# The down products of a feed-forward stage by one level of Strassen's scheme, with the weights streamed in order of use and all tiles at one remainder of 512 bytes

## The chip, the cores and the metric

One NeuronCore of a Trainium2 chip runs the kernel. The metric is the device time of one execution in microseconds; lower is better. TensorE multiplies, VectorE (DVE), ScalarE (ACT) and GpSimd (POOL) do the elementwise work, and SyncE (SP) issues the DMAs.

## The reference

Two decoder layers over 512 tokens of width 1024, in float32. Each layer is a mixer between two half-step SwiGLU feed-forward blocks, every block behind an RMS norm. The mixer is stick-breaking attention (16 heads of 64) in the first layer, and sliding-window attention with sinks and rotary angles in the second.

```
def swiglu(h, w_gate_up, w_down):
    gate, up = jnp.split(h @ w_gate_up, 2, axis=-1)
    return (jax.nn.silu(gate) * up) @ w_down
...
for i in range(DEPTH):
    x = x + 0.5 * swiglu(rms_norm(x, norm_gains[i, 0]), ffn_w_gate_up[i, 0], ffn_w_down[i, 0])
    h = rms_norm(x, norm_gains[i, 1])
    x = x + (stick_breaking_attention if i % 2 == 0 else sliding_window_attention)(h, ...)
    x = x + 0.5 * swiglu(rms_norm(x, norm_gains[i, 2]), ffn_w_gate_up[i, 1], ffn_w_down[i, 1])
```

The inner width of the feed-forward blocks is 2816, which is 22 tiles of 128; the model width is 8 tiles.

## The kernel before

Activations stand transposed: a tile holds 128 features on the partitions and the 512 tokens as columns. The eight tiles `x0` to `x7` hold the residual stream. Every float32 product is made of three passes in the type float32r: an operand is split exactly into a high part (a copy that rounds, on ACT) and a low part (what is left, by a subtraction on DVE), and `terms` issues high x high, high x low and low x high (line 75). The instructions on TensorE stay in the order of the program; the other engines' are ordered by a scheduler when the kernel is built.

The program runs six stages: feed-forward 0, stick-breaking attention, feed-forward 1, feed-forward 2, sliding-window attention, feed-forward 3. All weights form one stream in units of 8 tiles (7 for two in three of the down units). `_load` starts the DMA of a unit into one of three raw buffers (line 158), `_part` splits it (ACT on line 181, DVE on line 186, for some attention units POOL on line 184) into one of three pairs `whi` and `wlo`, and `release` goes on with the next unit when TensorE has used one.

A feed-forward stage (`ffn`) first goes over the 22 columns of 128 inner features. For each it makes two banks `gu` in PSUM, gate and up, each of 8 terms of 512 columns, and `swiglu` (lines 307 to 314) turns them into the parts `hh` and `hl`. Then come the down products: for each of the 8 output tiles one bank `dn` gathers 22 terms, in units of 8, 7 and 7; `residual` adds half of it to `x` (line 300), and `following` hands the tile to `norm_tile` of the next stage (lines 252, 253, 260 and 261: two parts of the tile times its gain, and its squares added to `acc`, by POOL for tiles 1 to 5 and by DVE for 6 and 7). After the last stage `following` stores the tile.

The tiles of the constants, of the weights and normalised activations, and of a stage lie one behind another in SBUF. Three small tiles `nv`, `nr`, `nt` of 16 bytes a partition, 32 in the placement, lie between the second group and the third. So weights and normalised activations begin at 96 bytes over a multiple of 512, and the tiles of the feed-forward and stick-breaking stages at 192.

Of the kernel before, what the change touches and what calls it, by code (L numbers as in the profile page):

```python
# [15 lines left out]
P = 128  # L16
T = 512
# [5 lines left out]
DOWN = (8, 7, 7)  # L23
# [13 lines left out]
NEG = -1.0e30  # L37
ROT = HD // 4
NROT = ROT // 2
# 500000 ** (-arange(0, 16, 2) / 16) in float32  # L40
# [24 lines left out]
class _Ordered:  # L65
    """an engine whose instructions stay in the order of the program"""
# [40 lines left out]

class _Trunk:
    def __init__(self, tc, pools, psum, aps):
        self.tc, self.nc = tc, _Engines(tc)  # L110
        self.const, self.work = pools
        self.psum = psum
        self.aps = aps
        self.units = []
        self.raw, self.ready = [], []
        self.taken = self.spent = 0
        self.roped = False
        self.extra = -1

# [7 lines left out]
    def terms(self, out, pairs, first=True, last=True, release=()):  # L127
# [4 lines left out]
        for i, ((wh, wl), (xh, xl)) in enumerate(pairs):  # L132
# [3 lines left out]
            if i in ((n - 1,) if release == 1 else release):  # L136
                self.release(1)
            yield cost

    def mm3(self, out, pairs, first=True, last=True, release=()):  # L140
        for _ in self.terms(out, pairs, first, last, release):
            pass
# [5 lines left out]
    def queue(self, ap, pool=False):  # L148
        self.units.append((ap, ap.shape[1], pool))

    def _load(self, pieces=1):
        n = len(self.raw)
        if n < len(self.units):
            ap = self.units[n][0]
            raw = self.work.tile([P, ap.shape[1]], F32, tag="raw", name=f"raw{n}", bufs=UNITS)
            self.raw.append(raw)
            if pieces == 1:
                self.nc.sync.dma_start(raw, ap)

    def _open(self, n):  # L160
        size = self.units[n][1]
        hi = self.work.tile([P, size], F32R, tag="whi", name=f"whi{n}", bufs=UNITS)
        lo = self.work.tile([P, size], F32R, tag="wlo", name=f"wlo{n}", bufs=UNITS)
        self.ready.append((hi, lo))

    def advance(self, hi, lo):
        """one more unit of the weight stream ahead, in tiles that the stage has free"""
        n = self.extra = len(self.ready)
        self.ready.append((hi, lo))
        self._part(n)  # L170
        self._load()

    def _part(self, n, i=0, pieces=1):
        nc, (ap, size, pool) = self.nc, self.units[n]
        size //= pieces
        s = slice(i * size, (i + 1) * size)
        hi, lo = self.ready[n]
        raw = self.raw[n]
        if pieces > 1:
            nc.sync.dma_start(raw[:, s], ap[:, s])  # L180
        nc.scalar.copy(hi[:, s], raw[:, s])  # L181
        if pool and pieces == 1:
            for t in (slice(0, size // 2), slice(size // 2, size)):
                nc.gpsimd.tensor_sub(lo[:, t], raw[:, t], hi[:, t])  # L184
        else:
            nc.vector.tensor_sub(lo[:, s], raw[:, s], hi[:, s])  # L186

    def release(self, count):
        self.spent += count
        ahead = UNITS + (self.spent <= self.extra)  # L190
        while count and len(self.ready) < min(self.spent + ahead, len(self.units)):
            n = len(self.ready)
            self._open(n)
            self._part(n)
            self._load()

    def weights(self, a):
        """the next unit of the stream as [row, a, column] high and low parts"""
        hi, lo = self.ready[self.taken]
        self.taken += 1  # L200
        h3, l3 = (t.rearrange("p (a b) -> p a b", a=a) for t in (hi, lo))
        return [(h3[:, i, :], l3[:, i, :]) for i in range(a)]

# [1 line left out]
    def setup(self, which):  # L205
# [10 lines left out]
        for n in range(UNITS):  # L216
            self._load(2)
            self._open(n)
        for half in range(2):
            for m in range(4):  # L220
                k = 4 * half + m
                nc.sync.dma_start(self.x[k], aps["xt"][k])
                if m < UNITS:
                    self._part(m, half, 2)
                self.norm_tile(k, which)
        for _ in range(UNITS):
            self._load()
        self.ident = c.tile([P, P], F32, name="ident")
# [15 lines left out]
    def norm_tile(self, k, which):  # L244
        nc, w = self.nc, self.work
        if k == 0:
            self.xh, self.xl = [], []
# [6 lines left out]
        self.xh.append(hi)  # L254
        self.xl.append(lo)
        if k == 0:
            nc.scalar.activation(self.acc, self.x[k], AF.Square)
        else:
            sq = w.tile([P, T], F32, tag="rbc", name="sq", bufs=1)
            nc.scalar.activation(sq, self.x[k], AF.Square)  # L260
            (nc.gpsimd if k < POOL_SQUARES else nc.vector).tensor_add(self.acc, self.acc, sq)  # L261
# [11 lines left out]
    def norm_rows(self):  # L273
# [4 lines left out]
        v = w.tile([P, TB], F32, tag="nv", name="nv", bufs=1)  # L278
        r = w.tile([P, TB], F32, tag="nr", name="nr", bufs=1)
        tmp = w.tile([P, TB], F32, tag="nt", name="nt", bufs=1)  # L280
# [17 lines left out]

    def residual(self, n, ps, factor):
        self.nc.vector.scalar_tensor_tensor(self.x[n], ps, factor, self.x[n], ALU.mult, ALU.add)  # L300

# [1 line left out]
    def swiglu(self, fp, f, gu):  # L303
        nc = self.nc
        g = fp.tile([P, T], F32, tag="g", name="g", bufs=2)
        u = fp.tile([P, T], F32, tag="u", name="u", bufs=2)
        nc.vector.tensor_mul(g, gu[0], self.rbc)  # L307
        nc.scalar.activation(g, g, AF.Silu)
        nc.vector.tensor_mul(u, gu[1], self.rbc)  # L309
        nc.vector.tensor_mul(u, g, u)  # L310
        hi = fp.tile([P, T], F32R, name=f"hh{f}")
        lo = fp.tile([P, T], F32R, name=f"hl{f}")
        nc.scalar.copy(hi, u)
        nc.vector.tensor_sub(lo, u, hi)
        return hi, lo

    def ffn(self, following, first=False, rope=False):
        tc, nc = self.tc, self.nc
        with tc.tile_pool(name="ffn", bufs=1) as fp:
            hs, evac = [], []  # L320
            xs = list(zip(self.xh, self.xl))
            ahead = []
            if first:
                ahead = [(self.bank("gu"), self.weights(KD)) for _ in range(3)]
                for half in range(2):
# [704 lines left out]
```

## Time and profile before

| | us |
|---|---|
| median of 3 runs | 1927.21 |
| lowest and highest run | 1924.83, 1928.83 |
| span of the profiled execution | 1925.5 |
| feed-forward 1: gate/up, down | 240.89, 123.21 |
| stick-breaking stage | 265.32 |
| sliding-window stage | 190.53 |

The span runs from the first to the last instruction. The page gives no device time for the profiled execution itself; its span lies inside the range of the three runs. The table's stages are stretches between the first matmuls of one kind and of the next. In the profile's rows, PE is TensorE's matmuls, PEld its weight loads; `gu<-xh,whi` reads: the bank `gu` was written from `xh` and `whi`. A matmul's length in a row is that of its pipeline; the distance of two starts is what it costs.

### The profile page before, as it was taken

The numbers are of one execution on the slowest core, as the hardware profiler recorded it, in microseconds if no ns is written. First come the engines' busy times: TensorE is split into PE (matmuls) and PEld (weight loads), VectorE is DVE, ScalarE is ACT, GpSimd is POOL, SyncE is SP. The second block draws the span as 40 slices with busy tenths as digits, with TensorE's granted clock in tenths as the row PEclk, the third lists the DMA queues.
The fourth block names the chain that finished last, engine by engine and source line by source line (L and its number), as shares of the span: only waits on it lengthen the run. The fifth ranks groups of instructions, "written<-read, shape, count | busy, mean of one in ns | idle before, by whom it ended". The sixth has DMA issues, their size and how long they took to land.

```text
span 1925.5 us, 22581 instructions
## 1 busy us (share of the span) xinstructions
PE 1895.7 (98%) x8994; PEld 1565.6 (81%) x8994; DVE 970.5 (50%) x1535; ACT 695.1 (36%) x1071; POOL 172.0 (9%) x131
## 2 busy tenths in 40 slices
PE   9999999999999999999999999999998999999999
PEld 7888888877887888888888888888887788888887
DVE  6444433378887644443235444423588664444321
ACT  5333222266675323332223333222357542223211
POOL 1000000233321000000000000000142210000000
PEclk9999999999999999999999999999989999999999
DMA  5233333321112333223333222333221122332331
GB/s 167 98 97 99 96 91 92 103 69 56 49 62 66 99 97 97 92 97 94 97 96 99 92 98 96 93 93 100 81 67 34 29 92 98 99 99 90 103 109 60
DMA packets 49930, 170.52 MB, mean 89 GB/s; under 512 B 5921, under 2 KB 6177, under 8 KB 49825
## 3 DMA queue, kind: packets, MB, share of 16 engines
q1 hardware_dynamic: 49824, 169.07, 27.9%
q8 instruction: 71, 1.16, 0.2%
q14 instruction: 35, 0.28, 0.0%
HBM read 166.96 MB, written 2.10 MB: 88 GB/s over the span
## 4 chain that ended last, share of the span: by engine, by line
PE 84%; DVE 8%; issue 4%; ACT 3%; POOL 1%; DMA 0%; SPq 0%; ACTq 0%; DVEq 0%; POOLq 0%
PE gu L75 49%; PE dn L75 23%; PE op L75 4%; PE tok L75 3%; DVE keep L459 2%; DVE beta L460 1%; PE pv L75 1%; DVE qs L376 1%; DVE wt L482 1%; ACT keep L453 1%; PE sc L75 1%; PE z L75 0%; PE ptr L75 0%; DVE e L793 0%; PE q L75 0%
## 5 line engine op out<-in xcount | busy, mean ns | idle before, releaser
L181 ACT CAST whi<-raw 128x1024 fp32r<-128x1024 f32 (+2 forms) x323 | 330.0, 1022 | 964.8 <-issue 361.6
L75 PE MATMUL gu<-xh,whi 128*128 128x512 f32 x1400 | 545.5, 390 | 1.4 <-ACT whi L181 1.4
L75 PE MATMUL gu<-xh,wlo 128*128 128x512 f32 x1400 | 545.0, 389 | 0.7 <-DVE wlo L186 0.7
L75 PE MATMUL gu<-xl,whi 128*128 128x512 f32 x1400 | 544.8, 389 | 0.5 <-DVE xl L253 0.5
L186 DVE TENSOR_TENSOR wlo<-raw,whi 128x1024 fp32r<-128x1024 f32 (+2 forms) x293 | 349.4, 1193 | 248.2 <-ACT whi L181 245.6
L75 PEld LDWEIGHTS gu<-xh,wlo 128*128 128x128 f32 x1400 | 262.8, 188 | 56.5 <-DVE wlo L186 1.8
L75 PEld LDWEIGHTS gu<-xh,whi 128*128 128x128 f32 x1400 | 262.9, 188 | 56.2 <-ACT whi L181 1.9
L75 PEld LDWEIGHTS gu<-xl,whi 128*128 128x128 f32 x1400 | 262.9, 188 | 55.3 <-DVE xl L253 0.9
L75 PE MATMUL dn<-hh,wlo 128*128 128x512 f32 x704 | 280.9, 399 | 0.0
L75 PE MATMUL dn<-hl,whi 128*128 128x512 f32 x704 | 277.4, 394 | 0.0
L75 PE MATMUL dn<-hh,whi 128*128 128x512 f32 x704 | 276.0, 392 | 0.0
L309 DVE TENSOR_TENSOR u<-gu,rbc 128x512 f32<-128x512 f32 x87 | 60.1, 691 | 274.7 <-PE gu L75 274.7
L75 PEld LDWEIGHTS dn<-hl,whi 128*128 128x128 f32 x704 | 132.1, 188 | 34.3
L75 PEld LDWEIGHTS dn<-hh,whi 128*128 128x128 f32 x704 | 132.2, 188 | 31.5
L75 PEld LDWEIGHTS dn<-hh,wlo 128*128 128x128 f32 x704 | 132.2, 188 | 30.5
L307 DVE TENSOR_TENSOR g<-gu,rbc 128x512 f32<-128x512 f32 x88 | 60.8, 691 | 176.5 <-PE gu L75 176.4
L261 POOL TENSOR_TENSOR acc<-acc,sq 128x512 f32<-128x512 f32 x30 | 46.4, 1547 | 1116.1 <-ACT sq L260 1116.1
L184 POOL TENSOR_TENSOR wlo<-raw,whi 128x512 fp32r<-128x512 f32 x60 | 87.5, 1483 | 164.9 <-ACT whi L181 164.9
L75 PE MATMUL tok<-whi,xh 128*128 128x256 f32 x288 | 86.4, 300 | 0.0
L75 PE MATMUL tok<-whi,xl 128*128 128x256 f32 x288 | 82.4, 286 | 0.1
L75 PE MATMUL tok<-wlo,xh 128*128 128x256 f32 x288 | 82.3, 286 | 0.1
L300 DVE SCALAR_TENSOR_TENSOR x<-dn,x 128x512 f32<-128x512 f32 x32 | 22.1, 691 | 116.5 <-PE dn L75 116.5
(310 smaller groups left out, 1957.4 us busy)
## 6 DMA issues: line engine op xcount, KB each, us to landing
raw<-in_gu_dram SPq DMA_DIRECT2D x173, 512.0 KB, 3.4
raw<-in_dn_dram SPq DMA_DIRECT2D x64, 448.0 KB, 3.3
raw<-in_dn_dram SPq DMA_DIRECT2D x32, 512.0 KB, 3.5
raw<-in_sbqk_dram SPq DMA_DIRECT2D x16, 512.0 KB, 3.4
raw<-in_swin_dram SPq DMA_DIRECT2D x10, 512.0 KB, 3.5
raw<-in_sbv_dram SPq DMA_DIRECT2D x8, 512.0 KB, 3.3
raw<-in_sbo_dram SPq DMA_DIRECT2D x8, 512.0 KB, 3.5
raw<-in_swo_dram SPq DMA_DIRECT2D x8, 512.0 KB, 3.3
```

The costliest lines, as they stand in the source:

```text
L75: return self._tc.keep_in_program_order(method(*args, **kwargs))
L181: nc.scalar.copy(hi[:, s], raw[:, s])
L184: nc.gpsimd.tensor_sub(lo[:, t], raw[:, t], hi[:, t])
L186: nc.vector.tensor_sub(lo[:, s], raw[:, s], hi[:, s])
L261: (nc.gpsimd if k < POOL_SQUARES else nc.vector).tensor_add(self.acc, self.acc, sq)
L300: self.nc.vector.scalar_tensor_tensor(self.x[n], ps, factor, self.x[n], ALU.mult, ALU.add)
L307: nc.vector.tensor_mul(g, gu[0], self.rbc)
L309: nc.vector.tensor_mul(u, gu[1], self.rbc)
L376: nc.vector.tensor_sub(out[other, h, :], src[own, :], out[own, h, :])
L453: nc.scalar.activation(keep[:, :, :n], z[:, :, :n], AF.Sigmoid, scale=-0.125)
L459: nc.vector.tensor_tensor_scan(rev, rev, rev, 1.0, ALU.mult, ALU.bypass)
L460: nc.vector.tensor_mul(beta[:, :, : n - 1], beta[:, :, : n - 1], keep[:, :, 1:n])
```

## The change

**Down products.** The inner tiles are taken in pairs, even and odd (11 pairs), the output tiles in pairs n and n + 4 (4 blocks), and the 512 tokens in two halves of 256. Each block is then a product of two-by-two matrices, for which Strassen's scheme (in Winograd's form) needs 7 products, where the plain form has 8. It needs sums: of the weights, four per block, made by POOL in `make_sums`; of the activations, three per pair, made by DVE in `swiglu`, which now writes seven operands per pair, high and low, each of 256 columns. The pairs are cut in two halves of the stage, `PAIRED = (6, 5)`: gate/up of 12 columns, down with 6 pairs, gate/up of 10 columns, down with 5 pairs. Each product's bank is added to a half of a tile of `x` as soon as it ends; products 1, 6, 7 and 4 of a block gather in one bank, and 5 and 3 in another, so that a product waits for the evacuation before it in its bank. `norm_tile` follows products 3 and 4 of a block in the second half.

**Stream.** DMA units are of 12 tiles (10 in the second half of a stage) in the order of use; splits are of 6 tiles (5) into one of `SLOTS = 4` slots. There are two raw buffers, and a third in feed-forward stages. `take` hands out single tiles, and `used` frees a slot. The first stage's first units are interleaved by tile, as the first matmuls want them.

**Placement.** The three small tiles move to the constants, and tiles of a few bytes are widened to 512 or put into one such line (`LINE`), so that every tile that TensorE reads from the weights, the normalised activations and a stage begins at one remainder of 512.

The core of the diff:

```diff
-DOWN = (8, 7, 7)
+TILES = 6
+SLOT = TILES * P
+RAWS, MORE_RAWS = 2, 1
+SLOTS = 4
+PAIRED = (6, 5)
+BLOCKS = KD // 2
...
+    def make_sums(self, g, t):
...
+        nc.gpsimd.tensor_add(s[0], a21, a22)
+        nc.gpsimd.tensor_sub(s[1], s[0], a11)
+        nc.gpsimd.tensor_sub(s[3], a12, s[1])
+        nc.gpsimd.tensor_sub(s[2], a11, a21)
...
+    def _split(self, n, s=slice(None), load=None):
...
+        self.nc.scalar.copy(hi, src)
+        if pool:
+            for h in (slice(0, t // 2 * P), slice(t // 2 * P, t * P)):
+                self.nc.gpsimd.tensor_sub(lo[:, h], src[:, h], hi[:, h])
+        else:
+            self.nc.vector.tensor_sub(lo, src, hi)
...
-        hi = fp.tile([P, T], F32R, name=f"hh{f}")
-        lo = fp.tile([P, T], F32R, name=f"hl{f}")
-        nc.scalar.copy(hi, u)
-        nc.vector.tensor_sub(lo, u, hi)
-        return hi, lo
+        if not odd:
...
+            part(0, 1, h[:, 0:1, :])
+            nc.vector.tensor_sub(t[:, 0, :], h[:, 1, :], h[:, 0, :])
+            part(1, 2, t[:, 0:1, :])
+        else:
...
+            part(2, 4, h)
+            nc.vector.tensor_sub(t[:, 1, :], h[:, 1, :], t[:, 0, :])
+            nc.vector.tensor_sub(t[:, 2, :], h[:, 1, :], he[:, 1, :])
+            nc.vector.tensor_sub(t[:, 3, :], h[:, 0, :], t[:, 1, :])
+            part(4, 7, t[:, 1:, :])
...
-            for n in range(KD):
-                ps = self.bank("dn")
-                at = 0
-                for size in DOWN:
-                    self.mm3(ps, list(zip(self.weights(size), hs[at : at + size])), first=(at == 0), last=(at + size == NF), release=1)
-                    at += size
-                self.residual(n, ps, 0.5)
-                following(n)
+    def down(self, pairs, following):
...
+        for n, p in down_order(BLOCKS):
+            out = bank(n, p)
+            j = (1, 5, 2, 3, 6, 7, 4).index(p)
+            first = p in (1, 2, 5)
+            w = self.take(pairs)
+            for i in range(pairs):
+                wh, wl, (slot, _) = w[i]
+                xh, xl = self.ops[i][j]
+                for m, (l, r) in enumerate(((wh, xh), (wh, xl), (wl, xh))):
+                    self.nc.tensor.matmul(out, l, r, ...)
+            for row, col, ps in {
+                1: ((0, 0, out),), 2: ((0, 0, out),), 6: ((0, 1, out),), 3: ((0, 1, out),),
+                7: ((1, 1, out),), 5: ((1, 1, out),), 4: ((1, 0, out),),
+            }[p]:
+                x = self.x[n + BLOCKS * row][:, col * W2 : (col + 1) * W2]
+                self.nc.vector.scalar_tensor_tensor(x, ps, 0.5, x, ALU.mult, ALU.add)
+            if following and p in (3, 4):
+                following(n + BLOCKS * (p == 4))
+            self.used(slot, pairs)
...
+def down_order(blocks):
+    out = []
+    for n in range(blocks):
+        out += [(n, 1), (n, 5)] + ([(n - 1, 4)] if n else []) + [(n, 2), (n, 6), (n, 3), (n, 7)]
+    return out[:-2] + [(blocks - 1, 7), (blocks - 1, 3), (blocks - 1, 4)]
```

Sums for block n + 1 are issued when the last split of block n is; a slot is freed at the end of the product that used it.

More of the change, by code (lines that the diff above doesn't have):

```diff
@@ L166, in advance @@
[L166 to L202, printed above, removed]
+    def queue(self, ap, sizes, pool=False, own=None, special=False):
+        n = len(self.loads)
+        self.loads.append((ap, own))
+        self.reads.append(len(sizes))
+        at = 0
+        for size in sizes:
+            s = slice(at * P, (at + size) * P)
+            self.plan.append((size, lambda s=s: self.raws[n][:, s], (n,), pool, None, special))
+            at += size
@@ L401, in project_pair @@
             ps = self.bank(nm)
-            yield from self.terms(ps, list(zip(self.weights(KD), xs)), release=1)
+            yield from self.terms(ps, list(zip(self.take(KD), xs)))
             if start:
@@ L1006, in layout @@
+    tiles = [t for cc in (CHUNKS, *range(CHUNKS)) for t in sw[cc]]
+    a["ww"] = stream(tiles + out_tiles(sw_w_out), "w")
     a["pos"] = c(np.asarray(positions).reshape(TB, P).T)
```

441 lines of the change are left out of this document (302 added, 139 removed).

## The prediction

> **What bounds the kernel now.** I read the page first (busy shares, then the chain that ended last), then the sums over stretches, cut where the matmuls change from one stage to the next.
>
> ```profile
> span 1925.5 us, 22581 instructions
> PE 1895.7 (98%) x8994; PEld 1565.6 (81%) x8994; DVE 970.5 (50%) x1535; ACT 695.1 (36%) x1071; POOL 172.0 (9%) x131
> PE 84%; DVE 8%; issue 4%; ACT 3%; POOL 1%; DMA 0%; SPq 0%; ACTq 0%; DVEq 0%; POOLq 0%
> ```
>
> TensorE is busy for 98% of the span and carries 84% of the chain; DVE is half idle and POOL nearly idle. The span lies 1.7 us under the median of the runs (1927.21), so I take differences from the trace and add them to the median. About 0.2% (3.9 us) is what a measurement of this kernel can tell from no change.
>
> ```profile
> core 0: us, PE busy (x) PEld busy (x) DVE busy (x) ACT busy (x) POOL busy (x), PEclk, DMA share, GB/s
> 250.32:373.54 123.22, 123.22 (x530) 99.12 (x529) 37.02 (x40) 32.92 (x40) 13.05 (x9) 1.00 0.31 92
> 1798.28:1921.49 123.21, 123.21 (x529) 98.93 (x527) 31.79 (x32) 22.12 (x23) 0.00 (x0) 1.00 0.30 89
> sum 492.85, PE 492.85 PEld 396.27 DVE 147.75 ACT 120.87 POOL 28.96; mean PE 123.21 PEld 99.07 DVE 36.94 ACT 30.22 POOL 7.24
> ...
> 1557.51:1798.28 240.77, 240.77 (x1068) 199.47 (x1066) 114.31 (x149) 74.74 (x94) 0.00 (x0) 1.00 0.30 96
> ```
>
> The first two rows are the first and the last of four down stretches, the sum is over the four; the last row is a gate/up stretch. PE is busy without a break in all of them at the full clock. A down stretch has 528 matmuls of 512 columns, 123.21/528 = 0.2333 us each. A gate/up stretch has 1056 and a few small ones, 0.227 us each. What TensorE has to do in these stages is their time; a gain there is a gain at the end.
>
> **The change part by part.** *Fewer products.* Per pair of output rows, 7 products of half width take the place of 8: 4 blocks x 7 products x 11 pairs x 3 passes = 924 matmuls of 256 columns per stage, 3696 in all, for 2112 of 512. The projections to token rows already run 256 columns with a new weight each time:
>
> ```profile
> 389.75 0.28 PE L75 MATMUL tok<-whi,xh 128*128 128x256 f32 x1
> 389.87 0.28 PE L75 MATMUL tok<-wlo,xh 128*128 128x256 f32 x1
> 389.99 0.28 PE L75 MATMUL tok<-whi,xl 128*128 128x256 f32 x1
> 390.11 0.28 PE L75 MATMUL tok<-whi,xh 128*128 128x256 f32 x1
> ```
>
> The starts stand 0.120 us apart (the 0.28 is the pipelined length). That is not half of 0.227: 2 x 0.120 - 0.227 leaves 0.013 us per matmul that does not shrink with the columns. So 3696 x 0.120 = 443.5 us against 492.85: -49.3, or 12.3 a stage. The ends are half of a down matmul, 0.1167 (-61.5), and half of the old down plus that 0.013, 0.130 (-12.4); I take 0.120, the row of the very shape. The Trainium skill, "TensorE: Matmul & The Clock Gate", section "Back-to-back issue gap", gives columns / 2.4 + 2.5 ns, 109 ns at 256: by that, as an estimate, the new down would be 403 us. The rows of this trace stand above it at both widths, and they decide.
>
> *Placement.* All tiles now begin at one remainder of 512 bytes. Before, weights and normalised activations share one (96) and run at 0.227, while the down products' activations lie at another (192) and run at 0.233. At one common remainder I leave gate/up at 0.227 and have counted 0.120 for down, whose row is of the equal kind. The 192 output-projection matmuls of the stick-breaking stage, also mixed, may gain as much as 0.0063 each: 0 to -1.2; I take -1.
>
> *New work on DVE, ACT and POOL.* Two output rows used to need 44 tiles of weights split into parts, in six splits, and two evacuations of 512 columns. Now they need, in each half, 7 splits (6 tiles wide in the first, 5 in the second: 77 tiles) and 7 evacuations of 256 columns, and POOL makes 4 sums for them.
>
> ```profile
> L186 DVE TENSOR_TENSOR wlo<-raw,whi 128x896 fp32r<-128x896 f32 x64 | 69.9, 1092 | 101.9 <-ACT whi L181 99.6
> L181 ACT CAST whi<-raw 128x896 fp32r<-128x896 f32 x64 | 60.3, 943 | 245.7 <-PE dn L75 217.6 <-PE gu L75 28.1
> L314 DVE TENSOR_TENSOR hl<-u,hh 128x512 fp32r<-128x512 f32 x88 | 60.4, 686 | 4.1 <-ACT hh L313 4.1
> L313 ACT CAST hh<-u 128x512 fp32r<-128x512 f32 x88 | 54.7, 621 | 62.1 <-DVE u L310 62.1
> L840 DVE TENSOR_TENSOR ol<-pv,oh 128x256 fp32r<-128x256 f32 x16 | 6.6, 415 | 7.4 <-ACT oh L839 7.4
> L686 POOL TENSOR_TENSOR q<-ra,rb 128x256 f32<-128x256 f32 x3 | 2.2, 738 | 0.2
> ...
> L184 POOL TENSOR_TENSOR wlo<-raw,whi x60: 1264/1298/2280, 364.9 to 1431.7; 128x512 fp32r<-128x512 f32 x60
> L253 DVE SCALAR_TENSOR_TENSOR xl<-x,gain,xh 128x512 fp32r<-128x512 f32 x7 | 5.2, 744 | 0.0
> ```
>
> Between 512 and 896 columns DVE takes 1.06 ns per column: 0.957 us for 768 (first half, six pairs), 0.821 for 640 (second, five). ACT's copies by its two rows: 0.84 and 0.73, under the 2.16 or 1.80 us of a product, so ACT is no bound. POOL by 256 (0.738) and 512 (median 1.298): 2.19 ns per column, 1.86 and 1.58 a sum. An evacuation: 0.415. POOL alone is no bound either: 4 x 1.86 = 7.4 us in the 15.1 of a block. But the two get in each other's way:
>
> ```profile
> 1465.16 1.89 POOL L810 TENSOR_TENSOR e<-e,st 128x1024 f32<-128x1024 f32 x1 [4.49 <-DVE st L809]
> ...
> 1465.57 2.56 DVE L186 TENSOR_TENSOR wlo<-raw,whi 128x1024 fp32r<-128x1024 f32 x1
> ```
>
> POOL ends at 1467.05, the split of 1024 columns only at 1468.13, 1.08 later; its own median is 1.22 (the row that follows). It waited for POOL's whole instruction and hid only some 0.14 of its start. Its maximum over 293 is that very 2.56, and POOL's row above has the same in its maximum (2.280 for 1.298).
>
> ```profile
> L186 DVE TENSOR_TENSOR wlo<-raw,whi x293: 678/1220/2559, 5.8 to 1907.0; 128x1024 fp32r<-128x1024 f32 x112, 128x896 fp32r<-128x896 f32 x32, 128x512 fp32r<-128x512 f32 x3
> ```
>
> The Trainium skill has this as a rule that speaks against the change: "SBUF — State Buffer", section "SBUF: two separate sides", makes the port pair of the two an exclusive lock when DVE has two SBUF inputs and POOL reads SBUF, held for the whole instruction. The trace agrees, but for the 0.14.
>
> So per block of the first half DVE has 7 x (0.957 + 0.415) = 9.6 us, and stands still for the part of POOL's 4 x 1.72 = 6.9 that no evacuation (they read PSUM: 2.9) covers: 13.6 in all, against 15.1 of TensorE. It holds. In the second half TensorE takes 7 x 15 x 0.120 = 12.6; DVE 8.65 + (5.8 - 2.9) = 11.5. It just holds, until blocks 1 and 2 add two normalised tiles each (DVE 0.744, POOL 1.298 less 0.14): + 1.5 + 2.3 = 15.3, or 2.7 over. Two such blocks: 5.4 us of stall in stages 0 to 2; the last stage stores instead and has none. What waits is the evacuation of product 6, queued on DVE behind splits that nobody needs yet, and product 7 writes the same PSUM tile.
>
> *Stalls at the ends of a half.* In the last block product 7 follows 6 at once. Its wait is an evacuation:
>
> ```profile
> 1921.26 0.40 PE L75 MATMUL dn<-hh,wlo 128*128 128x512 f32 x1
> ...
> 1921.69 0.69 DVE L300 SCALAR_TENSOR_TENSOR x<-dn,x 128x512 f32<-128x512 f32 x1 [13.57 <-PE dn L75]
> ```
>
> 0.43 from the start of the last matmul to DVE, less its own 0.12, plus 0.415: 0.75, with one restart 0.8; 1.6 a stage. At the head of a half, product 6 needs sums of the last odd column: on DVE two multiplications (1.4), the low part for product 2 (0.69), three differences (1.2), ACT's copy (0.84) and the last low part (0.96), 5.1 beside three splits (2.9) and up to two waits for POOL (3.4): 8 to 11.4, against three products and five sixths of the fourth, 8.3 in the first half and 6.9 in the second. I take 1.5 and 1.0 (0 to 4.5). Blocks that hold still lose some tenths when a split catches POOL: 1.0 a stage. Together 2.5 + 1.6 + 1.0 + 5.4 = 10.5 in stages 0 to 2, 5.1 in stage 3: **36.6** in all. The low end is 1.6 a stage (6.4), if the lead of three split slots absorbs the rest. The high end is 15 a stage (60): each second-half block 2.7 over, the head at 4.5.
>
> *Start.* The first weights now come tile by tile in the order of use.
>
> ```profile
> 5.85 0.67 PE L75 MATMUL gu<-xh,whi 128*128 128x512 f32 x1 [0.41 <-ACT whi L181]
> ...
> 8.03 0.50 PE L75 MATMUL gu<-xh,whi 128*128 128x512 f32 x1 [0.95 <-ACT whi L181]
> ...
> 9.14 0.50 PE L75 MATMUL gu<-xh,wlo 128*128 128x512 f32 x1 [0.37 <-DVE wlo L186]
> ...
> 10.44 0.50 PE L75 MATMUL gu<-xh,wlo 128*128 128x512 f32 x1 [0.35 <-DVE wlo L186]
> ```
>
> From 5.85 to 10.44 stand 8 matmuls worth 1.8 us, so 2.8 are lost; ACT and DVE still have their copies to do, and I take half, -1.4 (0 to -2.8).
>
> *Off the path.* SP issues fewer and larger transfers, 1.5 times 512 KB; its queue waits for free buffers now as then, and down draws 92 GB/s at a DMA share of 0.31 in the first row above. With three raw buffers in a feed-forward stage a block's pair is asked for some three products (5 to 6 us) before its sums:
>
> ```profile
> raw<-in_gu_dram SPq DMA_DIRECT2D x173, 512.0 KB, 3.4
> ```
>
> A landing took 3.4 us of that; if the cover went, a stall of up to a landing per block would show. The second swiglu of a pair is longer on DVE, under gate/up, where DVE is busy 114 of 241 us. In the attention stages the splits come in sixes for eights and POOL's in 384 columns for 512: 0, with +-4 for the fill rates, tuned to other unit sizes.
>
> Sum: -49.3 + 36.6 - 1.4 - 1 = -15.1, **1912 us**.
>
> **The rivals.** *The shared port decides (slower).* One mechanism, at one place: DVE's in-order queue in the second half of down, where splits wait for POOL's sums and hold the evacuation of product 6. At 15 a stage the sum is -49.3 + 60 - 2.4 = +8, 1935; the point from which it decides is (49.3 + 2.4)/4 = 12.9 us of stall a stage. For it: the 2.56 row, where the full wait is paid, and 15.3 against 12.6. Against it: DVE is 30% busy in down before, and three slots are ahead.
>
> *All is hidden.* Only 1.6 a stage remains: -49.3 + 6.4 - 2.4 = -45, 1882. For it: no row of down before shows an idle PE. Against it: POOL's busy time there goes from a mean of 7.24 us to some 55 a stage.
>
> *The fixed 0.013 us goes, or grows.* If the new common place of tiles takes it from gate/up's 4224 matmuls: -55 more, 1857. The skill's gap formula, cited above, is this case. If the common place costs what the mixed one does now, 0.0063 x 4224 = +27, 1939. The two equal-remainder kinds of the trace, at 96, speak for neither.
>
> *No change that can be told*, stall 11.9 to 13.9 a stage: 1923 to 1931.
>
> **How the numbers follow.** Forecast (stall 5 to 11.9 a stage, 1895 to 1923) 0.40; the port (1931 to 1950) 0.27; all hidden (1878 to 1895) 0.13; the fixed part gone 0.04 and grown 0.05; no change 0.11. Faster 0.40 + 0.13 + 0.04 = 0.57, slower 0.27 + 0.05 = 0.32, same 0.11. The range reaches into the hidden case and over most of the port's: 1882 to 1941. The forecast's own is 1895 to 1923.
>
> **What would show it.** Down matmuls should start 0.120 apart inside a product, gate/up's 0.227 as now. A half of down should last 60.5 or 50.4 plus its stalls: per stage some 121 in stages 0 to 2 and 116 in the last. Idle PE should be ended by DVE's evacuation ahead of product 7 and by the low part of the operands ahead of the first product 6; splits on DVE should average well over 0.957 and POOL's sums over 1.86 where they meet. The prediction is wrong if a second half of stages 0 to 2 lasts over 62 us, if its stalls end in DMA, or if gate/up's cadence moves.

## The result, and the profile after

The change made the kernel slower by about 1%, which is little but clear of the noise: 1947.36 us in the median of its runs against 1927.78 for the kernel before on the same chip, and a ratio of 1.0113 over the runs (95% interval 1.0096 to 1.013). The forecast was 1912. The profiled execution took 1953.03 with a span of 1951.3, 25.8 more than the span before; what follows is read from it. It is the longest of the four, and its granted clock was 0.982 where the other three had 0.986 to 0.988, so the slow running described below is probably more than in the others. One run of kernel 1 below took 3663.84 us for 1886.93 to 1900.09 of its other three, and its median leaves that run out.

The page of the changed kernel:

```profile
span 1951.3 us, 26890 instructions
...
PE 1871.1 (96%) x10578; PEld 1629.2 (83%) x10578; DVE 1376.7 (71%) x2208; ACT 830.7 (43%) x1384; POOL 439.5 (23%) x275
...
PE 80%; DVE 13%; ACT 3%; issue 3%; DMA 1%; POOL 0%; SPq 0%; ACTq 0%; DVEq 0%; POOLq 0%
```

TensorE still bounds the kernel, but DVE now carries 13% of the chain that ended last, for 8% before. Cut by stage, nearly all of the loss lies in down: its four stages together take 516.63 us with the tail of the last store, for 496.82 before (+19.8). The first stage's gate/up, with the start, gives +3.7 (253.99 us for 250.32), the sliding-window stage +2.0, the stick-breaking stage +0.2; gate/up elsewhere is the same within 0.1.

The stretches of the changed kernel; the first eight rows are the halves of down, two to a stage, and the last three are a closer look at the fourth (the eighth row ends with the store of the last tile):

```profile
core 0: us, PE busy (x) PEld busy (x) DVE busy (x) ACT busy (x) POOL busy (x), PEclk, DMA share, GB/s
145.16:210.91 65.75, 61.16 (x505) 60.61 (x504) 54.65 (x62) 24.30 (x30) 27.05 (x12) 1.00 0.27 93
319.74:381.29 61.55, 53.31 (x421) 52.18 (x420) 54.17 (x65) 27.77 (x41) 34.52 (x21) 0.97 0.24 79
778.90:845.99 67.09, 62.51 (x505) 61.95 (x504) 53.87 (x62) 24.31 (x30) 26.87 (x12) 0.97 0.27 92
954.82:1019.17 64.35, 56.32 (x421) 54.84 (x420) 56.80 (x68) 29.27 (x44) 31.12 (x17) 0.92 0.25 78
1151.19:1218.19 67.00, 62.42 (x506) 61.87 (x504) 54.23 (x62) 24.32 (x30) 27.01 (x12) 0.97 0.26 90
1327.02:1390.88 63.86, 55.55 (x421) 54.66 (x420) 57.34 (x68) 29.41 (x44) 30.23 (x17) 0.92 0.24 78
1715.40:1781.15 65.75, 61.17 (x505) 60.62 (x504) 53.67 (x62) 24.27 (x30) 26.87 (x12) 1.00 0.28 94
1889.98:1951.26 61.28, 54.25 (x421) 53.22 (x419) 45.79 (x60) 19.34 (x27) 21.99 (x12) 0.94 0.25 89
sum 516.63, PE 466.69 PEld 459.95 DVE 430.52 ACT 202.99 POOL 225.67; mean PE 58.34 PEld 57.49 DVE 53.82 ACT 25.37 POOL 28.21
...
1008.88:1012.24 3.36, 0.28 (x3) 0.11 (x2) 3.25 (x6) 2.15 (x4) 1.32 (x1) 0.99 0.00 0
1012.24:1015.65 3.41, 3.41 (x16) 3.41 (x17) 0.72 (x1) 0.00 (x0) 0.00 (x0) 0.51 0.65 231
1015.65:1019.17 3.52, 3.52 (x31) 3.52 (x31) 2.45 (x4) 2.43 (x4) 0.00 (x0) 1.00 0.17 33
```

A first half should last 504 x 0.120 = 60.5 us and a second 50.4. They last 65.8 to 67.1 and 61.3 to 64.4. Two things are in the difference. One is seen in the row from 1008.88: TensorE is busy for 0.28 of 3.36 us while DVE is busy for 3.25. The other is new: in the next 3.41 us TensorE is busy throughout, but PEclk is 0.51 and only 16 matmuls start, 0.213 apart, where the row after it has 31 in 3.52. Before, every down stretch had PEclk 1.00; now six of the eight halves are below.

I separated the two by the distances between the starts of the down matmuls: what a distance has over 0.120 is a gap if it is 0.2 us or more, else slow running. In the eight halves the gaps sum to 53.6 us and the slow running to 16.2. Eleven stretches of 3.41 us at half clock lie in these halves, 37.5 us in all.

Who ends the gaps, from the waits of TensorE (us in total, times, longest):

```profile
engine line waited for: us in total, times, longest us
PE dna L85 <- DVE x L542: 31.4, 22, 3.1
PE dna L85 <- DVE ops L436: 8.9, 4, 3.4
...
PE dna L85 <- ACT slot L282: 2.7, 3, 1.1
...
PE gu L85 <- DVE xl L370: 2.1, 2, 1.3
```

`dna` is the bank of products 1, 6, 7 and 4, `dnb` that of 2, `dnc` that of 5 and 3. L542 is the evacuation of a product, L436 the low part of the operands, L370 the normalised tile at the start; all of these are DVE's. L282 (ACT) and L287 (DVE) split the weights. The timeline at the head of the first half shows why DVE is late:

```profile
153.90 2.44 POOL L217 TENSOR_TENSOR s<-raw,s 128x768 f32<-128x768 f32 x1 [1.96 <-DVE slot L287]
...
154.89 2.27 DVE L287 TENSOR_TENSOR slot<-s,slot 128x768 fp32r<-128x768 f32 x1
155.20 2.32 PE L85 MATMUL dnc<-ops,slot 128*128 128x256 f32 x18
...
157.08 0.41 DVE L542 SCALAR_TENSOR_TENSOR x<-dnb,x 128x256 f32<-128x256 f32 x1
157.23 1.80 POOL L218 TENSOR_TENSOR s<-raw,rawx 128x768 f32<-128x768 f32 x1 [0.89 <-DVE slot L287]
157.41 2.44 DVE L287 TENSOR_TENSOR slot<-raw,slot 128x768 fp32r<-128x768 f32 x1
...
159.78 0.41 DVE L542 SCALAR_TENSOR_TENSOR x<-dna,x 128x256 f32<-128x256 f32 x1
...
160.34 1.90 PE L85 MATMUL dna<-ops,slot 128*128 128x256 f32 x14 [2.82 <-DVE x L542]
```

Two splits that take 0.95 alone take 2.27 and 2.44, because each starts inside a sum of POOL. The second stands ahead of the evacuation of product 6 on DVE. TensorE ended product 3 (`dnc`) near 157.3, and product 7, which writes the same tile as 6, could start only at 160.34.

### The profile page after: what moved, and what is told of

Its sections match the earlier page's. It is cut to its first block, busy times and chain, and to the rows that moved or that the text cites. A ratio compares the mean times of both kernels' runs of the same rounds, so it can differ in the third digit from the quotient of the medians.

```text
span 1951.3 us, 26890 instructions
## 1 busy us (share of the span) xinstructions
PE 1871.1 (96%) x10578; PEld 1629.2 (83%) x10578; DVE 1376.7 (71%) x2208; ACT 830.7 (43%) x1384; POOL 439.5 (23%) x275
## 3 DMA queue, kind: packets, MB, share of 16 engines
q1 hardware_dynamic: 36288, 169.07, 25.7%
## 4 chain that ended last, share of the span: by engine, by line
PE 80%; DVE 13%; ACT 3%; issue 3%; DMA 1%; POOL 0%; SPq 0%; ACTq 0%; DVEq 0%; POOLq 0%
PE gu L85 48%; PE dna L85 11%; PE dnc L85 4%; PE op L85 4%; DVE slot L287 4%; PE tok L85 3%; PE dnb L85 2%; PE pv L85 1%; DVE keep L640 1%; PE k L85 1%; DVE x L542 1%; DVE ops L436 1%; PE sc L85 1%; PE z L85 1%; ACT slot L282 1%
## 5 line engine op out<-in xcount | busy, mean ns | idle before, releaser
L85 PE MATMUL gu<-xh,slot 128*128 128x512 f32 x2800 | 868.2, 390 | 0.5 <-DVE slot L287 0.4
L85 PEld LDWEIGHTS gu<-xh,slot 128*128 128x128 f32 x2800 | 526.5, 188 | 112.1 <-DVE slot L287 2.1
L85 PE MATMUL gu<-xl,slot 128*128 128x512 f32 x1400 | 546.1, 390 | 2.1 <-DVE xl L370 2.1
L287 DVE TENSOR_TENSOR slot<-raw,slot 128x768 fp32r<-128x768 f32 (+2 forms) x270 | 288.1, 1068 | 165.1 <-ACT slot L282 162.7
L282 ACT CAST slot<-raw 128x768 fp32r<-128x768 f32 (+2 forms) x308 | 241.4, 785 | 363.9 <-PE gu L85 227.2
L85 PE MATMUL dna<-ops,slot 128*128 128x256 f32 x2112 | 284.4, 291 | 44.4 <-DVE x L542 31.4
L85 PEld LDWEIGHTS dna<-ops,slot 128*128 128x128 f32 x2112 | 271.8, 199 | 50.9 <-issue 25.5
L85 PEld LDWEIGHTS gu<-xl,slot 128*128 128x128 f32 x1400 | 263.5, 188 | 57.7 <-DVE xl L370 3.1
L287 DVE TENSOR_TENSOR slot<-rawx,slot 128x768 fp32r<-128x768 f32 (+1 forms) x112 | 128.6, 1148 | 74.6 <-ACT slot L282 73.9
L282 ACT CAST slot<-s 128x768 fp32r<-128x768 f32 (+1 forms) x128 | 99.9, 781 | 145.4 <-PE dna L85 85.1
L287 DVE TENSOR_TENSOR slot<-s,slot 128x768 fp32r<-128x768 f32 (+1 forms) x128 | 143.4, 1120 | 24.3 <-ACT slot L282 23.5
L282 ACT CAST slot<-rawx 128x768 fp32r<-128x768 f32 (+1 forms) x112 | 87.0, 777 | 140.7 <-PE gu L85 78.4
L85 PE MATMUL dnc<-ops,slot 128*128 128x256 f32 x1056 | 141.4, 289 | 0.0
L429 DVE TENSOR_TENSOR g<-gu,rbc 128x512 f32<-128x512 f32 x88 | 60.5, 687 | 35.9 <-PE gu L85 35.8
```

The lines of the kernel that those rows point to most:

```text
L85: return self._tc.keep_in_program_order(method(*args, **kwargs))
L282: self.nc.scalar.copy(hi, src)
L287: self.nc.vector.tensor_sub(lo, src, hi)
```

## The experiments

All times below are medians of a kernel's runs, with the ratio to the kernel before on the same chip, worked out over the runs; gaps and slow running are those of the eight down halves of the profiled execution, worked out as above. The expectations call the kernels by names: no_sums is 1, sums_on_dve 2, sums_in_pieces 3, sums_spread 5, spread_squares_order 6, gap_lengths 10.

| kernel | us | ratio (95% interval) | gaps | slow |
|---|---|---|---|---|
| the change | 1947.36 | 1.0113 (1.0096 to 1.013) | 53.6 | 16.2 |
| 1 no sums (work left out) | 1892.23 | 0.9829 (0.9796 to 0.9862) | 7.3 | 0.6 |
| 2 sums on DVE, in a row | 1935.67 | 1.0052 (1.0035 to 1.007) | 39.8 | 12.2 |
| 3 sums on POOL in pieces | 1933.70 | 1.0038 (1.0024 to 1.0053) | 37.5 | 13.5 |
| 4 another order of products | 1949.61 | 1.0118 (1.0103 to 1.0134) | 45.7 | 14.5 |
| 5 sums on DVE, spread | 1909.38 | 0.9914 (0.989 to 0.9938) | 20.4 | 2.3 |
| 6 as 5, squares on DVE, end of half | 1897.04 | 0.9849 (0.9828 to 0.987) | 11.9 | 3.4 |
| 7 before, aligned | 1915.10 | 0.9943 (0.9923 to 0.9962) | | |
| 8 the change with plain down | 1916.17 | 0.995 (0.9934 to 0.9967) | | |
| 9 POOL writes only (work left out) | 1892.11, one run | | 7.3 | 0.6 |
| 10, 12 gaps of chosen length | 1916.29, 1938.67, one run each | | 28.7, 45.5 | 5.2, 12.4 |
| 11 as 6, with 4's order | 1888.05 | 0.9805 (0.9782 to 0.9828) | 7.6 | 1.7 |

**1. No sums.** The four sums are left out, the splits that read them read tiles filled once a stage.

```diff
-        nc.gpsimd.tensor_add(s[0], a21, a22)
-        nc.gpsimd.tensor_sub(s[1], s[0], a11)
-        nc.gpsimd.tensor_sub(s[3], a12, s[1])
-        nc.gpsimd.tensor_sub(s[2], a11, a21)
...
+        s = [b[:, : t * P] for b in self.blank[1]]
```

> The four sums of a block are left out: the splits of products 5, 6, 3 and 7 read tiles that POOL fills once a stage, so DVE has every split and every evacuation and POOL only the squares (the products themselves are of other numbers). Theory A, the shared port (DVE stands still while POOL's sums run, its queue is in order, and the evacuation of product 6 comes late): the stalls of 16 to 21 us a stage fall to 2 to 4, and with them the half-speed stretches of the clock in down; 1890 to 1905 us. Theory B, DVE's own added splits and evacuations are too much for it: the stalls stay above 12 a stage, 1935 to 1947. Theory C, the clock falls by itself in 256-column work: half-speed stretches in down stay, 1920 or more.

Measured: 1892.23 us, as theory A has it; gaps 7.3 us, and no half-speed stretch in down. DVE's own work, which is all still there, does not make the gaps by itself. The page of this kernel, to be set against the change's row of the same kind that follows:

```profile
PE 1855.7 (98%) x10578; PEld 1618.6 (85%) x10578; DVE 1248.9 (66%) x2208; ACT 832.2 (44%) x1384; POOL 183.4 (10%) x163
...
L287 DVE TENSOR_TENSOR slot<-s,slot 128x768 fp32r<-128x768 f32 (+1 forms) x128 | 113.9, 889 | 39.2 <-ACT slot L282 38.7
```

The groups of the change itself:

```profile
L287 DVE TENSOR_TENSOR slot<-s,slot 128x768 fp32r<-128x768 f32 (+1 forms) x128 | 143.4, 1120 | 24.3 <-ACT slot L282 23.5
...
L542 DVE SCALAR_TENSOR_TENSOR x<-dna,x 128x256 f32<-128x256 f32 x128 | 53.3, 416 | 32.1 <-PE dna L85 31.5
```

The same 2208 DVE instructions are busy 1376.7 us with POOL's sums beside them and 1248.9 without: 128 us of standing still. A split of a sum takes 1120 ns for 889. The evacuations, which read PSUM, take 416 ns in the change and 421 without the sums, so they are not held.

**2. The sums on DVE.**

```diff
-        nc.gpsimd.tensor_add(s[0], a21, a22)
+        nc.vector.tensor_add(s[0], a21, a22)
```
(and so the other three)

> The four sums move from POOL to DVE, the order of all else unchanged. By the rows of the change's own trace DVE then has about 9.6 + 3.3 = 12.9 us in a block of the first half (15.1 of TensorE) and 8.6 + 2.7 = 11.3 in the second (12.6), 12.8 with two normalised tiles. Theory A (port): with no POOL beside it DVE keeps up but for tenths, stalls of 4 to 8 a stage, 1900 to 1915. Theory B (DVE's own load): 3 us more of it a block, so worse than the change, over 1950. Theory D, sums that come too late because of the weights' transfers, whoever makes them: about as the change, 1940 to 1950.

Measured: 1935.67, 12 under the change, where theory A asked for 1900 to 1915 and B for over 1950. Neither had it. First halves were cured but for one gap of 1.72 us; second halves of stages 0 to 2 kept a gap of 2.2 to 2.6 in each of the first three blocks, always ahead of product 7. So POOL's hold is not needed for the delay: four sums of DVE's own, 3 to 3.5 us of work close together ahead of the evacuation, do it as well. At the heads of the halves this stands alone: each of the four takes 0.81 or 0.95 there. In blocks 1 and 2 of stage 0's second half one of the four takes 1.92 beside a square that POOL adds, so there a hold has a share.

**3. The sums in pieces on POOL.**

```diff
+        def cut(op, out, x, y, step=2 * P):
+            for at in range(0, t * P, step):
+                op(out[:, at : min(at + step, t * P)], x[:, at : min(at + step, t * P)], y[:, at : min(at + step, t * P)])
...
```
(and each of the four sums goes through `cut`)

> Each sum stays on POOL and is cut into instructions of 256 columns (three for 768 and for 640). Theory A (port): a DVE instruction now waits for a piece of some 0.75 us instead of a whole sum of 1.8, so single waits halve; but more DVE instructions meet a piece, and POOL's own time grows to about 2.2 a sum. The evacuation of product 6 comes 1 to 2 us earlier: 1920 to 1938. Theory D (late sums): the sums take longer, the same or worse than the change, 1947 to 1960.

Measured: 1933.70, inside theory A's range. TensorE's waits for evacuations fell from 31.4 to 12.9 us; 13.1 us of waits for slots took part of their place. In the one that I followed, ahead of product 2 of block 2 in stage 0, the split stood on ACT behind a square that had waited 4.12 us for POOL, whose queue the pieces lengthen; that the others are of the same kind is not shown.

**4. Another order.** From the second block on, product 6 ahead of 2, so that two products stand between 6 and 7.

```diff
-        out += [(n, 1), (n, 5)] + ([(n - 1, 4)] if n else []) + [(n, 2), (n, 6), (n, 3), (n, 7)]
+        out += [(n, 1), (n, 5)] + ([(n - 1, 4), (n, 6), (n, 2)] if n else [(n, 2), (n, 6)]) + [(n, 3), (n, 7)]
```

> Only the order of products changes: from the second block on, 6 goes ahead of 2, so that 2 and 3 stand between 6 and 7, and in the last block 2 stands between 6 and 7 where nothing stood. Theory A: DVE's lag of 2 to 4 us is the same but product 7 comes one product (1.8 to 2.2 us) later, so the waits on the evacuation (31 us in all) fall to under half and the half-speed stretches behind them with it: 1925 to 1937. A theory by which PE waits for weight slots or operands rather than the evacuation: no change, 1945 to 1950.

Measured: 1949.61, no gain; my expectation of 1925 to 1937 fell, and the waits on the evacuation went only from 31.4 us to 26.3. The gap ahead of the last block's product 7 went (0.8 to 3.2 us before), but a new one of 2.20 appeared in three second halves ahead of product 4 of block 2, and the heads, where most of the loss is, kept theirs. The burst had moved on to the next evacuation. In the profiled execution down did get 9.6 us shorter (507.1 for 516.6), but the attention stages, which the edit does not touch, were 6.6 longer (464.7 for 458.1); so the order's own worth is smaller than what those stages can move by, and this kernel does not settle it.

**5. The sums on DVE, one at a time.** Each sum is issued behind an evacuation; the sums' total is that of kernel 2.

```diff
+        for _ in range(1 if self.spread else 4):
+            self.pending.pop(0)()
...
+            if self.pending:
+                self.pending.pop(0)()
             self.used(slot, pairs)
```
(`pending` holds the four sums; `spread` is set while `down` runs)

> The four sums are on DVE and, from the second block of a half on, issued one at a time, each behind an evacuation, where sums_on_dve issued all four in a row ahead of one. DVE's work is the same. Theory A' (it is the burst of 3 us ahead of the evacuation in DVE's in-order queue, by POOL's hold or by DVE's own sums, that makes product 7 late): the gaps of 1.7 us in first halves and 2.2 to 2.5 in every block of second halves shrink under 1 us, no half-speed stretch follows in down, 1892 to 1908. Theory B (DVE is full: some 12.8 us of work in 12.6 in second halves): second halves stay 8 or more us over, 1925 to 1936.

Measured: 1909.38, at the upper end of A'. The longest waits for an evacuation in kernel 2 and here:

```profile
PE dna L85 <- DVE x L542: 32.7, 21, 2.4
```

```profile
PE dna L85 <- DVE x L550: 17.2, 20, 1.2
```

About as many waits, but no gap over 1.41 us, and no half-speed stretch in down. The slow running fell from 12.2 to 2.3. The sums still wait for the weights' transfers as before, so sums that come too late (theory D of experiment 2) are not what made the gaps. The same work in another place in one engine's queue is worth 26 us.

**6 and 11. A version that beats both.** Kernel 6 also adds the squares of the normalised tiles on DVE and puts product 2 between 6 and 7 in the last block; kernel 11 also takes the order of kernel 4.

```diff
-POOL_SQUARES = 6
+POOL_SQUARES = 1
...
+    n = blocks - 1
+    return out[:-4] + [(n, 6), (n, 2), (n, 7), (n, 3), (n, 4)]
```

> As sums_spread, and two things more: the squares of the normalised tiles are added on DVE (0.57 to 0.68 us each) and not on POOL (1.3 us, for which DVE's two-input work stands still), and in the last block of a half product 2 stands between 6 and 7. Theory A: the start loses its half-speed stretch (-3 to -4 us), the ends of the halves their 0.8 to 1.2 us (-6 in all), the normalised tiles of second halves their waits: 5 to 12 us under sums_spread, 1882 to 1900. Theory B (DVE full): more work on DVE makes it slower than sums_spread.

> As spread_squares_order, and from the second block on product 6 stands ahead of 2, so that two products stand between 1 and 6, 6 and 7, 7 and 4. The gaps of 0.7 to 1.15 ahead of product 7 in blocks 1 and 2 of second halves (3 halves, about 1.6 us each) go: 4 to 6 us less, 1890 to 1895. If DVE's total work and not its order sets them, they move to another product and the time stays at 1897.

Measured: 1897.04 and 1888.05, both in or under what was expected. Kernel 11 is 2.0% faster than the kernel before (0.9782 to 0.9828). The start has no half-speed stretch: 134.06 us from the first gate/up product to the first down product, for 139.88 in the change. The down halves of kernel 11:

```profile
139.35:199.87 60.52, 60.52 (x506) 60.52 (x504) 49.79 (x74) 24.40 (x30) 0.00 (x0) 1.00 0.29 102
308.70:361.38 52.68, 51.07 (x421) 50.55 (x420) 48.10 (x83) 28.92 (x43) 3.94 (x4) 1.00 0.27 92
...
1281.59:1334.09 52.50, 51.05 (x421) 50.52 (x420) 49.84 (x85) 28.99 (x43) 0.00 (x0) 1.00 0.29 95
...
sum 456.30, PE 446.54 PEld 444.18 DVE 388.62 ACT 203.80 POOL 3.94; mean PE 55.82 PEld 55.52 DVE 48.58 ACT 25.47 POOL 0.49
```

First halves run without a gap, second halves with 1.4 to 2.5 us, all at the full clock. The order that brought nothing in kernel 4 pays here, once no burst follows it.

**7. The kernel before, aligned.** `nv`, `nr`, `nt` become constants; nothing else is edited. The weights and normalised activations move with them, from a remainder of 96 to that of the stage's tiles, 192.

```diff
+        self.small = [c.tile([P, TB], F32, name=nm) for nm in ("nv", "nr", "nt")]
...
+        v, r, tmp = self.small
```

> The kernel before, with the three 16-byte tiles of the norm moved to the constants, so that weights, normalised activations and the down products' activations share one remainder of 512 bytes (the window stage's own tiles stay mixed). If the remainders make the 0.233 of down's matmuls, they go to 0.227: 2112 x 0.0064 = 13.5 us less, with the output projection's 192 some 1 more, 1911 to 1916. If something else makes it, 1924 to 1930.

Measured: 1915.10, as expected. A stretch of down:

```profile
252.06:371.74 119.68, 119.68 (x530) 99.13 (x528) 37.02 (x40) 33.01 (x40) 13.07 (x9) 1.00 0.31 95
```

119.68/528 = 0.2267, for 0.2333: three small tiles made 3.5 us a stage.

**8. The change with plain down.** Stream, placement and start of the change, 528 matmuls of 512 columns a stage.

```diff
-                self.down(pairs, following if half else None)
+            for n in range(KD):
+                ps = self.bank("dn")
+                for i in range(NF):
+                    self.mm3(ps, [(*self.take(1), hs[i])], first=(i == 0), last=(i == NF - 1))
+                self.residual(n, ps, 0.5)
+                following(n)
```

> The changed kernel without Strassen's products: the stream in order of use, the aligned tiles and the new start stay, the feed-forward stages compute down as before (512 columns, 22 terms a row, weights in units of 6 tiles). Down at 0.227 throughout and no stall: 119.8 us a stage against 123.2. If the placement is the only gain and the start's 3.7 us stays, 1914 to 1920; if the stream itself costs or brings something elsewhere, outside of that.

Measured: 1916.17, in the range, and not to be told from kernel 7. So no gain of the stream shows here, and the start's +3.7 and the window stage's +2.0 are there without Strassen's products too (253.8 and 192.5 us, as in the change). Against this kernel Strassen's products cost the change 31 us; kernel 11, with the squares moved too, is 28 under it.

**9. POOL writes only.**

```diff
+        for j in (0, 1, 3, 2):
+            for _ in range(2):
+                nc.gpsimd.memset(s[j], 0.0)
```
(in place of the four sums)

> In place of each of the four sums POOL fills the same tile twice with zeros: it is as busy at the same places (two fills of some 0.75 us for a sum of 1.86), but reads nothing of SBUF and waits for no weights (the sums are left out, so products 5, 6, 3 and 7 compute other numbers). If DVE stands still only while POOL reads SBUF, splits fall back to a mean near 0.89 and the gaps to those of no_sums (0.8 to 1.2 a half), 1890 to 1902. If any POOL instruction holds DVE, the splits stay over 1.05 and the time is 1925 to 1940.

The page of this kernel:

```profile
PE 1851.0 (98%) x10578; PEld 1615.7 (85%) x10578; DVE 1249.4 (66%) x2208; ACT 832.4 (44%) x1384; POOL 344.6 (18%) x403
...
L217 POOL MEMSET s<- 128x768 f32 (+1 forms) x256 | 174.5, 687 | 1169.5 <-DVE slot L286 1141.6
...
L286 DVE TENSOR_TENSOR slot<-s,slot 128x768 fp32r<-128x768 f32 (+1 forms) x128 | 113.8, 889 | 42.5 <-ACT slot L281 41.8
```

POOL is busy at the same places for 174.5 us, and DVE's 2208 instructions take 1249.4 us, as with no sums at all. So it is POOL's reading of SBUF that holds DVE, not its being busy and not its writes. The Trainium skill, "SBUF — State Buffer", section "SBUF: two separate sides", says just that of a DVE instruction with two SBUF inputs; the runs agree on both sides of it, with 889 and 1120 ns.

**10 and 12. Gaps of chosen length.** Kernel 5 with 1, 3, 5 and 7 extra DVE instructions ahead of the evacuation of the last block's product 6, by stage.

```diff
+                if (n, p) == (BLOCKS - 1, 6):
+                    for _ in range(2 * int(self.stage) + 1):
+                        self.nc.vector.scalar_tensor_tensor(idle[:, 1, :], out, 0.5, idle[:, 0, :], ALU.mult, ALU.add)
```
(kernel 12; in kernel 10 the instruction read idle tiles alone)

> As sums_spread, with 1, 3, 5 and 7 extra DVE instructions of 256 columns (about 0.4 us each, on idle tiles) ahead of the evacuation of product 6 in the last block of both halves of stages 0, 1, 2 and 3. The gaps ahead of product 7 become about 1.2, 2.0, 2.8 and 3.6 us in first halves, some 0.6 more in second. Theory: a window of 3.41 us with 2 us or more of idle TensorE is followed by a window at half speed, one with 1.8 or less is not, wherever the windows happen to stand; so stage 0 shows none, stage 3 one in each half but the very last, stages 1 and 2 according to how the gap falls on the windows. Rival: the clock falls by chance or by load, and then the stretches don't follow the added gaps.

Kernel 10 told nothing of the gaps: the scheduler put the extra instructions into idle time of DVE earlier in the half, and the gap ahead of product 7 stayed at 0.77 in first halves. In kernel 12 they have to follow product 6.

> As gap_lengths, but the 1, 3, 5 and 7 extra DVE instructions read the PSUM tile of product 6 beside an idle tile, so that they can't move ahead of product 6's end and product 7 must wait for all of them. The gaps ahead of the last block's product 7 become about 1.2, 2.0, 2.8 and 3.6 us in the first halves of stages 0 to 3 and up to 0.6 more in the second. Theory (a free-running window of 3.41 us with 2 us or more of idle TensorE is followed by one at half speed, with 1.8 or less by none): stage 0 shows no half-speed stretch behind its last block's gap, stages 1 and 2 one where 2 us of the gap fall into one window, stage 3 nearly always; each stretch costs some 1.7 us. Rival (the clock falls by chance or by load): the stretches don't follow the gaps' lengths.

The eight gaps became 1.10, 1.71, 2.62, 3.37, 3.54, 4.28, 4.46 and 3.84 us, from stage 1 on longer than expected. The stretch of 3.41 us behind five of them:

```profile
198.60:202.01 3.41, 3.41 (x29) 3.41 (x30) 1.33 (x3) 0.73 (x1) 0.00 (x0) 1.00 0.44 177
366.90:370.31 3.41, 3.41 (x28) 3.41 (x29) 0.42 (x1) 0.83 (x1) 1.79 (x3) 1.00 0.64 235
826.80:830.21 3.41, 3.41 (x18) 3.41 (x18) 0.08 (x1) 0.08 (x1) 0.00 (x0) 0.50 0.02 6
997.50:1000.91 3.41, 3.41 (x19) 3.41 (x18) 1.38 (x2) 0.83 (x1) 0.00 (x0) 0.51 0.02 9
...
1758.60:1762.01 3.41, 3.41 (x19) 3.41 (x18) 0.24 (x1) 0.24 (x1) 0.00 (x0) 0.50 0.00 0
```

Full clock behind the two short ones, half clock behind the other six, the three not shown included. The rival, chance, would not sort eight gaps so.

## Why the prediction was wrong, step by step

The step that failed is the stalls' term, +36.6: the gaps it stands for measured 53.6, and 16.2 us of slow running at half clock came on top, for which the sum had no term. With 53.6 in its place the prediction's own sum would come to about 1929, no gain; with the clock and the start it comes to a loss.

**Right: the matmuls.** Down matmuls start 0.120 apart and gate/up's 0.227, as taken: 443.5 us of products stand in the eight halves. The -49.3 is there in full. The placement's share of it, 0.2333 to 0.227, is kernel 7.

**Wrong: the stalls' size, +36.6.** The gaps measure 53.6. By the terms of that sum: the heads of the halves, taken as 2.5 a stage, measure 9.1, 8.2, 8.3 and 8.0 (33.5 in all for 10): 1.32 and 2.98 ahead of products 6 and 7 of block 0 in first halves, and 3.7 to 4.8 in second halves, most of it inside the first products, which wait for the last pair's operands. In first halves both waits are for evacuations, of products 1 and 6, and not, as the prediction had it, for operands. The prediction's own working gave 8 to 11.4 us of DVE's work against 6.9 to 8.3 of TensorE's and then took a value near the lower end; the rows it had spoke for the upper. It also counted only product 6 and not 7, which stands behind the same queue. The ends of the halves, taken as 1.6 a stage, measure 10.7 in all for 6.4. The overrun in blocks 1 and 2, 5.4 a stage, measures 3.2, 2.8, 3.4 and none (9.4 for 16.2). The tenths, 4, did not show.

**Missing: the clock.** No term held the 16.2 us of slow running, nor the start's. Nor did any rival, so the high end of 15 a stage was passed with 17.4, where the gaps alone are 13.4.

**Wrong: the start.** -1.4 was taken, +3.7 came: the order of use did not help, since TensorE waits there for normalised tiles on DVE (2.1 us), which POOL's squares hold up, and a half-speed stretch of 6.83 us follows. The two can be told apart: kernel 12, with the squares on POOL and the same start, fell into no half-speed stretch there. From its first gate/up product to its first down product it takes 137.31 us, for 139.88 in the change and 134.06 in kernel 11, which has the squares on DVE. So, by one profile of each, the half clock cost the change's start some 2.6 us, which another run can be without, and the squares on POOL some 3.2.

**The rest.** The attention stages moved by +2.2, inside the +-4. Together: -49.3 + 53.6 + 16.2 + 3.7 + 2.2, less 0.7 of a shorter tail and of rounding, is +25.7, and 25.8 was measured.

**The rivals.** *The shared port decides* came true as a mechanism, but not as it was placed: it was to decide in second halves alone, and the first halves' heads lose 4.3 each. Its band of 1931 to 1950 holds the 1947, but by luck: by its own sum the measured gaps give some 1929, and the clock and the start make up the rest. Kernels 1 and 9 show that without the sums 7.3 us of gaps remain, near the 6.4 of *all is hidden*; both took 1892 for the 1882 of that rival, whose difference is mostly the start and the attention stages. The signs named beforehand were right: TensorE's waits ended with DVE's evacuation ahead of 7 and the operands' low part, splits averaged 1.07 to 1.15 us, POOL's sums 1.7 to 2.3, and two of three second halves of stages 0 to 2 lasted over the mark of 62. The prediction named DVE's in-order queue, but sized it by the total work of a block (13.6 us in the 15.1 of a first-half block: it holds). What decides is the longest run of work ahead of an evacuation: kernel 5 gives DVE more to do than kernel 1 and all of kernel 2's work, and loses 20.4 us where kernel 2 loses 39.8.

Left open: how much of the window stage's +2.0 is half-speed windows that fall elsewhere in each run. That stage took 190.5 to 195.9 us over these kernels, and the stick-breaking stage 263.5 to 269.9, so differences of a few us between two kernels' single profiles are not down's alone.

## What to carry to other kernels

When an engine's queue feeds a bank that TensorE needs soon, ask how long the longest run of other work ahead of that evacuation can be, not whether the engine's total fits; then spread that work one piece behind each evacuation. Take two-input work from POOL wherever DVE is on the path: a sum took DVE 0.88 us in the mean (768 and 640 columns), where POOL took 1.7 to 2.3 and held DVE's other work meanwhile: the 128 us of standing still are 1.0 for each of the 128 sums, more than the sum costs on DVE itself. And a gap of TensorE has two prices: 2 us or more of idleness may cost some 1.7 us again, so several gaps of 1 us, well apart, are better than one of 3.

## What was not expected of the hardware

**The clock halves behind a gap, by fixed windows.** In each trace the half-speed stretches begin on one grid of 3.413 us, whose place differs from run to run. I took all windows of that grid that lie wholly in feed-forward stages, behind the start, in eleven kernels (the change, 1 to 6 and 9 to 12), with the clock full in them, and left out those at the program's end. In 38 the clock halved in the next window; they held 1.99 to 3.41 us of idle TensorE, counted by the distances between matmul starts as above. In 4377 it did not; they held at most 1.83, but for one with 2.03. So a gap of 3 us that falls across two windows can pass: the gap of 2.98 at the head of the first half was free in stages 0 and 3 and brought a half-speed window in stages 1 and 2. The Trainium skill, "TensorE: Matmul & The Clock Gate", section "What's actually happening", has the free-running window of 3413 ns and the return to half clock after an idle window, and its section "Why this matters for your kernels" advises no gaps over about 3 us. The traces agree on the window; on the gap they differ: 2 us in one window were enough.

**Remainders.** A matmul of 512 columns whose two operands lie at different remainders of 512 bytes (96 and 192) takes 0.2333 us, at equal ones 0.2267, shown by kernel 7, whose gate/up stays as it was (240.8 us a stage in both kernels, with its operands at 96 before and at 192 in kernel 7). Two pairs of places are all that these runs have; that other unequal remainders cost the same is not shown.
